# The small products of a mixer: from fifteen steps to five ordered groups per unit

## The chip, the core and the metric

The kernel runs on one core of a Trainium2 chip. A core has a matrix engine (TensorE, PE in the profile, with its weight loads as PEld), a vector engine (VectorE, DVE), a scalar engine (ScalarE, ACT), GpSimd (POOL) and SyncE (SP), which issues most DMAs. The engines run side by side and wait for one another through semaphores; each takes its own instructions in the order in which they were queued. The metric is the time of one execution on the device in microseconds (us), given as the median of several runs.

## What is computed

One step of a one-layer encoder on 1024 frames of a new stream (the prompt) and 32 frames of a running one (the sample). After a norm and an input projection, a mixer with three kinds of heads follows, then an output projection and a convolutional feed-forward part. The change lies in the mixer. Cut to what matters (L is 64 frames, 32 for the sample):

```python
# six heads of kind GLA (dk 32) and five of kind HGRN2 (dk 64), dv 64: per chunk of L frames
b = cumsum(log_a)
scores[i, j] = sum_d q[i, d] * k[j, d] * exp(b[i, d] - b[j, d])     # j <= i
o = scores @ v + (q * exp(b)) @ S
S = exp(b_last) * S + (k * exp(b_last - b)).T @ v
...
# five heads of kind mLSTM (dk 64): per chunk
s = (q @ k.T) * w                                                  # w: stabilised decays
num, den = s @ v + w0 * (q @ C), sum(s) + w0 * (q @ n)
C, n = dc * C + (wk * k).T @ v, dc * n + sum(wk * k)
```

## The kernel before

The 1056 frames are cut into nine units: units 0 to 7 are 128 prompt frames each (two chunks of 64), unit 8 is the 32 sample frames. Three groups of units, (0, 1, 2), (3, 4, 5) and (8, 6, 7), go through `inproj` (L357) one after the other. Its large products are done in three passes with the operands split into a high and a low half (`mm3`, L100 to L103, so that these three lines stand for all large products). The mixer of a group's units (`mixer`, L722) is a generator; `merge` (L1654) takes steps of it between the steps of the next group's `inproj`, and those of the last group between the steps of `outproj` (L1027). So the small products of a mixer lie between large products of another part, and NMIX (L1667) tells `merge` how many steps of a mixer to count for each unit. The yields inside `mixer` are these steps.

The instructions are put in order at build time by a planner: for each engine it takes, among those that it holds to be ready, the one with the lowest place in the program. `tc.high_priority(offset=n)` sets an instruction's place n lower than where it was written; the helper `first` (L718) does this with AHEAD = 100 for nearly all small products, which therefore all carry the line L720 in the profile. `tc.issue_after(ins)` queues the instructions of its block behind `ins` on that engine; it sets an order and adds no wait. In the profile, then, a small product is known by its output tile and not by its line.

A unit goes through these steps. (1) The loads. (2) qz (the queries times exp(b)), dec and kh (keys of the state update), and four transposes of kh through the tile mi into kt2 (L794 to L800). (3) One step for each of six levels c = 32, 16, 8, 4, 2, 1 (L825; five levels for unit 8): the scores between the two halves of each block of 2c frames. A level takes a difference and two exponentials into x (L836 to L845, NX = 3 buffers), products into Ld and Qz (L841 to L853, two buffers each), 16 matmuls into the PSUM tile sc (L856 to L863, one buffer of two banks), and a masked copy into P (`put`, L810; an ACT copy for the first level). With the last level go the four products of the diagonal (sd, L873 to L876). (4) The state update: for each chunk eleven products into mi (`up`, L882 to L893). (5) The outputs: P times v and qz times S into og and oh (L896 to L907). (6) `finish` (L917): norm and gate. (7) The mLSTM scores (sm, L937 to L947). (8) Transposes of its keys (kp, L950 to L958, into kw2) and the update of C (um, L963 to L972). (9) Its outputs: oi and om (L976 to L981), then division, `finish` and the store.

In PSUM, mi is one bank in two halves that `small` (L243) hands out in turn; the tiles og, oh, sm, om and oi share two buffers (tag "o"); the large products share three banks (tag "big", pool psb).

A product of 64 rows and 64 columns takes a quarter of the 128x128 array; the profile writes this as `64*64`, rows by columns of the array. The small products have these shapes: sc `64*64` (the first level `64*32`), kh, sd and the first kp `128*128`, up `128*32` (GLA) and `128*64` (HGRN2), og and oh `64*64` with P and `128*64` with S, sm `128*64` and `64*64`, the last kp `64*128`, um and oi `128*64`, om `64*64`. Each product of a 32-bit tile, transposes apart, stands in the profile as two instructions.

Two more places are touched. `back` (L448) in `vg_across` turns blocks of the last group's projection with transposes, for one unit at a time. `rows` (L550) makes the row factors of the mLSTM and turns them into columns (L599 to L622), in pieces from the tile mi for the second and third group.

Of the kernel before, what the change touches and what calls it, by code (L numbers as in the profile page):

```python
# [91 lines left out]
def body(ctx: ExitStack, tc: tile.TileContext, a: dict):  # L92
# [264 lines left out]
    def inproj(g, xh, xl, normed, scaled=None):  # L357
# [88 lines left out]
        def vg_across(blks):  # L446

            def back(blk, fs, part):  # L448
                for (u, off, n) in units_of(g)[part]:
                    ps = psb.tile([128, 256], F32, tag="big", name=f"pb{u}_{blk}")  # L450
                    for e in range(2):
                        pe.transpose(ps[:n, 128 * e:128 * e + 128], fs[e][:, off:off + n], ident)
                    vg_store(blk, u, off, n, ps)

            before = None
            for blk in blks:
# [3 lines left out]
                for e in range(2):  # L460
                    ps = psb.tile([128, T], F32, tag="big", name=f"pv{g}_{blk}_{e}")
                    for k in range(8):
                        mm3(ps, [w[:, 128 * e:128 * e + 128] for w in ws[k]], (xh[:, k, :], xl[:, k, :]), k == 0, k == 7)
                    act.copy(fs[e], ps)
                    if before:
                        back(*before, slice(e, 1 + 2 * e))
                    yield
                before = (blk, fs)
                yield
            for e in range(2):  # L470
                back(*before, slice(e, 1 + 2 * e))
# [78 lines left out]
        def rows():  # L550
# [48 lines left out]
            own = psm.tile([128, 4, 128], F32, tag="o", name="rows0", bufs=2) if g == 0 else None  # L599
            dcp = small(3, 8) if g else own[:, 3, :24].rearrange("p (a b) -> p a b", b=8)  # L600
            for f in range(3):
                pe.matmul(dcp[:, f, :ci], self_[R, 128 * f:128 * f + 128], dc[R, :ci], start=True, stop=True)
            dcs = mx.tile([128, 3, 8], F32, tag="dcs", name=f"dcs{g}", bufs=2)
            cl = mx.tile([128, 3, 128], F32, tag="cols", name=f"cols{g}", bufs=2)
            if g:
                with tc.high_priority(offset=AHEAD):
                    act.copy(dcs[:, :, :ci], dcp[:, :, :ci])
            for i0, i1 in ((0, 3),) if g == 0 else ((0, 2), (2, 3)):
                if g:
                    yield  # L610
                pt = own[:, :3] if g == 0 else small(i1 - i0, 128)
                for i in range(i0, i1):
                    u, off, n = us[i]
                    pe.transpose(pt[:n, i - i0, :], st[:, off:off + n], ident)
                n = us[i0][2]
                with tc.high_priority(offset=AHEAD):
                    act.copy(cl[:n, i0:i1], pt[:n, :i1 - i0])
                for i in range(i0, i1):
                    cols_of[us[i][0]] = cl[:, i]
            if g == 0:  # L620
# [97 lines left out]
    def first(fn, *args, **kw):  # L718
        with tc.high_priority(offset=AHEAD):
            fn(*args, **kw)  # L720

    def mixer(u, g, ci0):  # L722
# [71 lines left out]
        for f0 in (0, 2):  # L794
            kps = small(2, 128)
            for f in (f0, f0 + 1):
                first(pe.transpose, kps[:n, f - f0, :], khf[:, f * n:f * n + n], ident)
            for ch, (o, m) in enumerate(chunks):
                with tc.high_priority(offset=AHEAD):
                    act.copy(kt2[o:o + m, ch, 128 * f0:128 * f0 + 256], kps[o:o + m].rearrange("p f n -> p (f n)"))  # L800
# [23 lines left out]
        li = 0  # L824
        for c in levels:  # L825
# [20 lines left out]
            li += 1  # L846
# [7 lines left out]
            sc = psm.tile([128, 1024], F32, tag="sc", name=f"sc{u}_{c}", bufs=1)  # L854
            sc = sc[:, :11 * SCW].rearrange("p (h s) -> p h s", s=SCW)
            for j in range(4):  # L856
                for (o, m) in chunks:
                    for hf in range(2):
# [3 lines left out]
                        first(pe.matmul, sc[o:o + mm, p0:p0 + q1 - q0, :m // 2], L[r, f, o:o + mm],  # L862
                              Q[r, q0:q1, o // 2:(o + m) // 2], start=True, stop=True)  # L863
            if c == levels[0]:
                for (o, m) in chunks:
                    act.copy(P[o:o + c, :, c:2 * c], sc[o:o + c, :, :c])
            else:
                put(c, sc[:n, :, :cl // 2])
            if c == 2:

                z = mx.tile([128, 512], F32, tag="x", name=f"x{u}_0", bufs=NX)
                dve.tensor_tensor(z[:, :4 * n], q4.rearrange("p f n -> p (f n)"), k4.rearrange("p f n -> p (f n)"), op=ALU.mult)
                sd = small(11)  # L873
                for f in range(4):
                    first(pe.matmul, sd[:n], z[:, f * n:f * n + n], of_head[:, f, :], start=f == 0, stop=f == 3)
# [3 lines left out]

        og = psm.tile([128, 6, 64], F32, tag="o", name=f"og{u}", bufs=2)  # L880
        oh = psm.tile([128, 5, 64], F32, tag="o", name=f"oh{u}", bufs=2)
        Ss = []  # L882
        for ch, (o, m) in enumerate(chunks):
            S = state["S", u == 8]
            Ss.append(S)
            up = small(4, 64)
            for (f, r0, dk, vc) in HEADS:
                first(pe.matmul, up[r0:r0 + dk, f, :], kt2[:n, ch, 128 * f + r0:128 * f + r0 + dk], v[:n, vc:vc + 64],
                          start=True, stop=True)
            Sn = mx.tile([128, 4, 64], F32, tag="S", name=f"S{u}_{ch}", bufs=3)  # L890
            dve.tensor_tensor(Sn, S, dec[:, :, ch:ch + 1].broadcast_to([128, 4, 64]), op=ALU.mult)
            si = dve.tensor_tensor(Sn, Sn, up, op=ALU.add)
            state["S", u == 8] = Sn  # L893
        yield

# [1022 lines left out]
```

## Time and profile before

| | |
|---|---|
| three runs | 1376.77, 1379.4 (median), 1380.69 us |
| the profiled execution | 1378.88 us |
| its span, first to last instruction | 1377.1 us |
| granted TensorE clock, mean | 0.989 |
| instructions of PE | 11472 matmuls |

The profile's page has, for each engine, the busy time and its share of the span; the span in 40 slices; the DMA queues; the chain of work that ended last; and the costliest groups of instructions. Views of the trace answer narrower questions: the instructions in order of time, the groups within a window, what an engine waited for, and the busy time by stage. The mixers' products lie between 153 and 650 us; what follows (the feed-forward part) isn't touched. A matmul's duration is its time from issue to the end of its results, and matmuls overlap: what one costs the engine is read from the starts of those that follow it.

### The profile page before, as it was taken

The page shows a single profiled execution, that of the slowest core. Times are in us where ns is not written, and L with a number is a line of the kernel's source. Part 1 is how long each engine was busy: PE and PEld are TensorE (multiplying, and loading weights), DVE is VectorE, ACT ScalarE, POOL GpSimd, SP SyncE. Part 2 cuts the span into 40 slices and gives each one's busy share as a digit, 9 for nine tenths or more (in the row PEclk, how much of TensorE's full clock was granted, in tenths as well). Part 3 has the DMA queues.
Part 4 walks back from the last instruction along what each step waited for, and adds up shares of the span by engine and source line. Part 5 has one row for each costly group of instructions (what it writes and reads, how often), then busy time and mean ns, then how long its engine had stood idle before and what let it go on. Part 6 is the DMA issues. An engine that isn't in the chain of part 4 may idle for free.

```text
span 1377.1 us, 29219 instructions
## 1 busy us (share of the span) xinstructions
PE 1326.5 (96%) x11472; PEld 1198.8 (87%) x11472; DVE 1029.4 (75%) x1916; ACT 705.0 (51%) x1369; POOL 313.1 (23%) x529
## 2 busy tenths in 40 slices
PE   6999999999999898999989999999999999999997
PEld 5999889898889786867879999999999997678885
DVE  4786458768587669685989888888888876399566
ACT  4555447445475547342665555555455545454552
POOL 5532411226012154222211112111121110010005
PEclk9999999999999999999999999999999999999998
DMA  9699778876789936543423565655374239744435
GB/s 342 203 318 363 262 243 284 260 262 207 262 261 316 336 96 198 176 130 88 168 66 116 163 177 136 150 141 156 107 184 129 87 113 394 274 152 133 147 110 123
DMA packets 125825, 269.72 MB, mean 196 GB/s; under 512 B 24007, under 2 KB 59367, under 8 KB 125607
## 3 DMA queue, kind: packets, MB, share of 16 engines
q1 hardware_dynamic: 111959, 245.43, 52.9%
q0 software_dynamic: 8928, 18.09, 7.1%
q10 hardware_dynamic: 4800, 4.33, 0.9%
q8 instruction: 90, 1.47, 0.4%
q14 instruction: 48, 0.39, 0.1%
HBM read 206.72 MB, written 86.18 MB: 213 GB/s over the span
## 4 chain that ended last, share of the span: by engine, by line
PE 75%; DVE 10%; DMA 6%; ACT 5%; issue 2%; POOL 1%; SPq 1%; DVEq 0%; ACTq 0%; POOLq 0%
PE pux L101 4%; PE pux L102 4%; PE pux L103 4%; PE pv L101 4%; PE pv L103 4%; PE pv L102 4%; PE puw L102 3%; PE puw L103 3%; PE puw L101 3%; PE q L101 3%; PE q L102 3%; PE q L103 3%; PE x L101 2%; PE x L102 2%; PE x L103 2%; PE zp L101 2%
## 5 line engine op out<-in xcount | busy, mean ns | idle before, releaser
L1341 DVE SCALAR_TENSOR_TENSOR y<-uu,fconv_sb,y 128x1060 f32<-128x1060 f32 x88 | 116.2, 1321 | 36.7 <-ACT y L1339 35.8
L1277 ACT COPY c<-pux 128x272 f32<-128x272 f32 (+1 forms) x132 | 49.3, 376 | 50.1 <-PE pux L103 46.5
L101 PE MATMUL pv<-wt_0h,xh 128*128 128x256 f32 (+2 forms) x195 | 57.7, 296 | 5.4 <-ACT xh L321 4.8
L1339 ACT ACTIVATE y<-uu,fconv_sb 128x1060 f32<-128x1060 f32 x44 | 56.1, 1274 | 12.1 <-POOL uu L1335 10.8
L101 PE MATMUL zp<-woh,ch 128*128 128x512 f32 (+1 forms) x144 | 59.4, 414 | 2.4 <-DVE z L1156 1.2
L1338 POOL COPY fhalo<-uu 128x2 f32<-128x2 f32 x44 | 17.1, 388 | 184.2 <-DVE uu L1282 184.2
L102 PE MATMUL zp<-wol,ch 128*128 128x512 f32 (+1 forms) x144 | 57.9, 402 | 0.0
L103 PE MATMUL zp<-woh,cl 128*128 128x512 f32 (+1 forms) x144 | 57.8, 402 | 0.0
L103 PE MATMUL pv<-wt_1h,xl 128*128 128x256 f32 (+2 forms) x195 | 57.1, 293 | 0.0
L103 PE MATMUL pv<-wt_0h,xl 128*128 128x256 f32 (+2 forms) x195 | 56.7, 291 | 0.4 <-DVE xl L322 0.4
L101 PE MATMUL pv<-wt_1h,xh 128*128 128x256 f32 (+2 forms) x195 | 56.9, 292 | 0.0
L102 PE MATMUL pv<-wt_1l,xh 128*128 128x256 f32 (+2 forms) x195 | 56.8, 291 | 0.0
L102 PE MATMUL pv<-wt_0l,xh 128*128 128x256 f32 (+2 forms) x195 | 56.2, 288 | 0.1
L1517 POOL TENSOR_TENSOR gss<-gss 128x1 f32<-128x1 f32 (+1 forms) x9 | 8.1, 899 | 186.8 <-ACT gjk L1510 186.8
L220 POOL TENSOR_SCALAR hrs<-hss 128x5 f32<-128x5 f32 (+3 forms) x27 | 9.6, 356 | 161.2 <-DVE hss L922 159.8
L101 PEld LDWEIGHTS pv<-wt_0h,xh 128*128 128x128 f32 (+1 forms) x195 | 36.8, 189 | 7.4 <-ACT xh L321 5.7
L431 POOL TENSOR_TENSOR vg<-vth,gh 128x256 f32<-128x256 f32 (+1 forms) x36 | 29.2, 812 | 61.6 <-DMA vm<-v_d 22.0
L815 DVE COPY_PREDICATED P<-masks_sb,sc 128x352 f32<-128x352 int32 (+1 forms) x44 | 29.8, 677 | 11.8 <-PE sc L720 11.5
L851 DVE TENSOR_TENSOR Qz<-x,qe 128x128 f32<-128x128 f32 (+1 forms) x106 | 29.8, 298 | 11.7 <-PE sc L720 11.0
L103 PEld LDWEIGHTS pv<-wt_0h,xl 128*128 128x128 f32 (+1 forms) x195 | 37.1, 190 | 1.2 <-DVE xl L322 0.9
L101 PEld LDWEIGHTS pv<-wt_1h,xh 128*128 128x128 f32 (+1 forms) x195 | 37.6, 193 | 0.4 <-issue 0.2
L103 PEld LDWEIGHTS pv<-wt_1h,xl 128*128 128x128 f32 (+1 forms) x195 | 37.4, 192 | 0.6 <-issue 0.2
(1718 smaller groups left out, 5384.3 us busy)
## 6 DMA issues: line engine op xcount, KB each, us to landing
wrP<-in_w_dn SPq DMA_DIRECT2D x27, 512.0 KB, 3.4
h_d<-y SPq DMA_DIRECT2D x22, 530.0 KB, 2.8
ht<-h_d SPq DMA_DIRECT2D x22, 530.0 KB, 8.8
wt_0r<-in_w_tok SPq DMA_DIRECT2D x21, 512.0 KB, 5.2
wt_1r<-in_w_tok SPq DMA_DIRECT2D x21, 512.0 KB, 6.8
ws_d<-in_w_dn POOLq DMA_DIRECT2D x20, 512.0 KB, 8.7
wrP<-ws_d SPq DMA_DIRECT2D x20, 512.0 KB, 4.2
wt_0l<-lt_d SPq DMA_DIRECT2D x14, 512.0 KB, 4.1
```

What stands on the lines that cost most here:

```text
L101: pe.matmul(ps, lh[0], rh[0], start=first, stop=False, **kw)
L102: pe.matmul(ps, lh[0], rh[1], start=False, stop=False, **kw)
L103: return pe.matmul(ps, lh[1], rh[0], start=False, stop=last, **kw)
L220: pool.tensor_scalar(out, ss, 1.0 / width, eps, op0=ALU.mult, op1=ALU.add)
L431: pool.tensor_tensor(o[:n], th[:n], gh[:n, c0:c0 + 256], op=ALU.mult)
L815: dve.copy_predicated(dst, mk.broadcast_to([n, 11, *mk.shape[2:]]), src)
L851: dve.tensor_tensor(Qp[:, 2 * i, :, :n // 2].rearrange("p e (m c) -> p e m c", c=c), second(x4[:, f:f + 1], c).broadcast_to([128, 2, n // ...
L1277: kept[name] = act.copy(t, ps)
L1338: behind["POOL"] = pool.tensor_copy(fhalo[:, j, :], u[:, NCOL - 2:NCOL])
L1339: act.activation(y, u, AF.Identity, scale=fconv[:, j, 2:3], bias=fconv[:, j, 3:4])
L1341: dve.scalar_tensor_tensor(y, uu[i][:, s:s + NCOL], fconv[:, j, s:s + 1], y, op0=ALU.mult, op1=ALU.add)
L1517: pool.tensor_tensor(ss[:n, 0:1], ss[:n, 2:3], ss[:n, 3:4], op=ALU.add)
```

## The change

Each unit's small products are queued in five groups, each a chain in a fixed order. `soon` replaces `first`: its offset is 400, and each product is queued behind the product before it. Two levels share one tile sc, and the level that is made last comes first; its results are stored side by side (`at`). With the first pair of levels go the transposes of kh, with the second the mLSTM's scores and key transposes, with the third the diagonal and the state update of both chunks; then og and oh with the update of C; then oi and om. The yields of a unit fall from fifteen to nine, and NMIX from 17 to 11. `back` turns all three units of a block at once, in two PSUM tiles; `rows` does its products in one piece in a tile of its own in all groups.

```diff
-            def back(blk, fs, part):
-                for (u, off, n) in units_of(g)[part]:
-                    ps = psb.tile([128, 256], F32, tag="big", name=f"pb{u}_{blk}")
+            def back(blk, fs):
+                us = units_of(g)
+                whole = psb.tile([128, 2, 256], F32, tag="big", name=f"pb{us[0][0]}_{blk}")
+                rest = psb.tile([128, 256], F32, tag="big", name=f"pb8_{blk}")
...
+            own = (psb if g else psm).tile([128, 4, 128], F32, tag="big" if g else "o", name=f"rows{g}", bufs=3 if g else 2)
...
-    def first(fn, *args, **kw):
-        with tc.high_priority(offset=AHEAD):
-            fn(*args, **kw)
+    SOON = 400
+    line = [None]
+    def soon(fn, *args, **kw):
+        with tc.high_priority(offset=SOON), tc.issue_after(line[0].ins) if line[0] else ExitStack():
+            line[0] = fn(*args, **kw)
...
+        def scores(sc, c, L, Q, at):
+            for j in (3, 0, 1, 2):
...
+                        soon(pe.matmul, sc[o:o + mm, p0:p0 + q1 - q0, at:at + m // 2], L[r, f, o:o + mm],
+                             Q[r, q0:q1, o // 2:(o + m) // 2], start=True, stop=True)
...
+        for l0 in range(0, len(levels), 2):
+            pair = [operands(c, i) for i, c in enumerate(levels[l0:l0 + 2])]
+            last_pair = pair[-1][0] == levels[-1]
+            if last_pair:
                 z = mx.tile([128, 512], F32, tag="x", name=f"x{u}_0", bufs=NX)
...
+            if l0 == 2:
+                act.copy(mqz[0:64, 0:5:2, :n], mq[0:64, :, :])
...
+            sct = psm.tile([128, 1024], F32, tag="sc", name=f"sc{u}_{l0}", bufs=1)
...
+            line[0] = None
+            for i in reversed(range(len(pair))):
+                scores(sc, *pair[i], i * (cl // 2))
+            sd = sct[:, 11 * SCW:11 * SCW + 11]
+            if l0 == 0:
+                keys()
+            elif l0 == 2:
+                memory_scores()
+            if last_pair:
                 for f in range(4):
-                    first(pe.matmul, sd[:n], z[:, f * n:f * n + n], of_head[:, f, :], start=f == 0, stop=f == 3)
+                    soon(pe.matmul, sd[:n], z[:, f * n:f * n + n], of_head[:, f, :], start=f == 0, stop=f == 3)
+                si = states()
+            for i, (c, L, Q) in enumerate(pair):
...
+                    put(c, sc[:n, :, at:at + cl // 2])
...
         og = psm.tile([128, 6, 64], F32, tag="o", name=f"og{u}", bufs=2)
         oh = psm.tile([128, 5, 64], F32, tag="o", name=f"oh{u}", bufs=2)
...
+        line[0] = None
...
+        memories()
...
+        line[0] = None
+        for h in range(5):
+            for ch, (o, m) in reversed(list(enumerate(chunks))):
+                soon(pe.matmul, oi[o:o + m, h, :], mqz[:, h, o:o + m], Cs[ch][:, h // 2, :], start=True, stop=True)
...
-    NMIX, NIN = 17, 12 + 2 + 24
+    NMIX, NIN = 11, 12 + 2 + 24
```

The functions `keys`, `memory_scores`, `states` and `memories` hold the lines of before for kt2, for sm with w and kp, for `up` with S, and for um with C; the products of both chunks come first in the last two, and the sums on VectorE behind them.

207 lines of the change are left out of this document (98 added, 109 removed).

## The prediction, made before the changed kernel ran

> **What bounds the kernel now.** I read the page first, for the engine that is full and for the chain that ended last:
>
> ```profile
> span 1377.1 us, 29219 instructions
> PE 1326.5 (96%) x11472; PEld 1198.8 (87%) x11472; DVE 1029.4 (75%) x1916; ACT 705.0 (51%) x1369; POOL 313.1 (23%) x529
> ...
> PE 75%; DVE 10%; DMA 6%; ACT 5%; issue 2%; POOL 1%; SPq 1%; DVEq 0%; ACTq 0%; POOLq 0%
> ```
>
> PE is busy for 96% of the span, and three quarters of the chain are its own work. [...] So the second view is the stages in which mixers run, and in them the small products alone:
>
> ```profile
> core 0: us, PE busy (x) PEld busy (x) DVE busy (x) ACT busy (x) POOL busy (x), PEclk, DMA share, GB/s
> 150.00:350.00 200.00, 195.86 (x2307) 179.31 (x2305) 142.20 (x330) 107.95 (x221) 52.02 (x76) 0.98 0.76 250
> 350.00:500.00 150.00, 144.46 (x1892) 129.71 (x1890) 106.65 (x284) 82.53 (x193) 32.01 (x52) 0.99 0.83 274
> 500.00:660.00 160.00, 152.77 (x1551) 118.77 (x1550) 120.37 (x258) 69.66 (x157) 51.70 (x80) 0.98 0.47 145
> ...
> 150.00:660.00 510.00, 141.14 (x3485) 112.42 (x3485) 0.98 0.69 224
> ```
>
> The last row is L720 alone: 3485 small products fill 141 of 510 us. In all three stages PE is idle for 2 to 5% of the time, VectorE for 25 to 29%. A microsecond of PE taken out of these 510 should therefore mostly come off the end, as long as the others can follow.
>
> What a small product costs isn't its duration, since many lie beside one another; it is read from the starts in the list of instructions in time. Here is one level of scores between large products (columns: start and duration in us, engine, line, operation, output from inputs, rows by columns of the array, size of the output, count):
>
> ```profile
> 305.60 0.28 PE L101 MATMUL pv<-wt_0h,xh 128*128 128x256 f32 x1
> 305.81 0.69 PE L720 MATMUL sc<-Qz,Ld 64*64 64x64 f32 x32
> 306.43 0.39 PE L102 MATMUL pv<-wt_0l,xh 128*128 128x256 f32 x1
> 306.66 0.28 PE L103 MATMUL pv<-wt_0h,xl 128*128 128x256 f32 x1
> 306.78 0.28 PE L101 MATMUL pv<-wt_0h,xh 128*128 128x256 f32 x1
> ```
>
> Large products follow each other by 0.12 us (306.66 to 306.78). From 305.60 to 306.66 pass 1.06 us; less two large steps of 0.12, the 32 products of the level cost 0.82 us. The first of them comes 0.21 us after the large one before it, and the second large one 0.23 us after the first: both edges are slow. A place where two shapes alternate gives the price of an edge:
>
> ```profile
> 598.55 0.56 PE L720 MATMUL om<-vm,w 64*64 64x65 f32 x10
> 599.04 0.56 PE L720 MATMUL mi<-vm,kw 128*64 128x65 f32 x10
> 599.53 0.33 PE L720 MATMUL om<-vm,w 64*64 64x65 f32 x2
> 599.79 0.33 PE L720 MATMUL oi<-C,mqz 128*64 128x65 f32 x2
> 600.05 0.33 PE L720 MATMUL om<-vm,w 64*64 64x65 f32 x2
> ```
>
> Ten products of one shape take 0.49 us, two take 0.26 us, each with one change of shape. Eight products more cost 0.23 us, 29 ns each, so the change alone costs 0.26 - 0.06 = 0.20 us. The level of scores gives a little less: four `64*64` products lie side by side where `128*64` has two, so 32 cost 32 x 14.5 ns = 0.46 us, and 0.82 - 0.46 leaves 0.18 us for each of its two changes. I take **0.18 us for a change of shape**, and keep 0.20 as the upper end.
>
> [...]
>
> **The change, part by part.** *Changes of shape.* Before, I counted them in the list in time. The second unit's mixer runs between these rows:
>
> ```profile
> 232.93 0.55 PE L720 MATMUL sc<-Qz,Ld 64*32 64x64 f32 x32
> 233.41 0.44 PE L101 MATMUL pf<-xh,wf_11h 128*128 128x384 f32 x1
> ...
> 284.67 0.64 PE L720 MATMUL oi<-C,mqz 128*64 128x65 f32 x16
> 285.24 0.39 PE L102 MATMUL pv<-wt_1l,xh 128*128 128x256 f32 x1
> ```
>
> with 37 changes, the third's from 289 to 343 us with 40, and between 150 and 660 us there are 353 with a mixer's product on at least one side: 39 a unit over nine units. After, from the code: the first group is `64*64`, `64*32`, `128*128` (three changes, since transposes have the shape of the large products). The second is `64*64` for both levels, `128*64` and `64*64` (sm), `128*128` and `64*128` (kp): six. The third is `64*64`, `128*128` (sd), and `128*32`, `128*64` twice (up): seven. The fourth is `64*64`, then `128*64` for S and um together: three. The fifth is `128*64`, `64*64`: three. That is 22 a unit, 198 in all, and 155 fewer: 155 x 0.18 = **27.9 us**.
>
> *Broken groups.* The planner puts a large product in between wherever an item of the chain isn't ready. sm needs two ACT copies, up needs kt2, qz times S needs the state after the first chunk. That the level made last comes first means that both are ready when the chain begins, and oi begins with the chunk whose C is late. No row shows how often groups break. It lies between no extra change and all 17 saved in a unit; I take three a unit, nearest to the clean count: 27 x 0.18 = **4.9 us** given back.
>
> *Waits of PE.* The places where PE, at a small product, waits for an engine:
>
> ```profile
> its engine sat idle before it (us, times) until:
>   issue: 14.9, 70
>   DVE Qz L851: 4.8, 7
>   DVE kh L793: 3.2, 2
>   DVE P L815: 2.8, 7
>   DVE kw L957: 2.7, 6
> ```
>
> The four rows with a name sum to 13.5 us in 22 waits. I leave them as they are (0), with half gained (7 us) and the slow rival below as the two ends.
>
> *Order on the other engines.* Nothing is added to VectorE or ScalarE; the work on w, kw2 and C moves ahead of the last levels and of `finish`. On VectorE that is (behind the bar: busy us in all, mean ns of one, then its idle time)
>
> ```profile
> L957 DVE TENSOR_TENSOR kw<-mi,cols 64x256 f32<-64x256 f32 (+1 forms) x8 | 2.6, 319 | 4.9 <-PE mi L720 4.9
> ...
> L947 DVE TENSOR_TENSOR w<-w,sm 128x320 f32<-128x320 f32 x2 | 1.0, 480 | 0.0
> ```
>
> four of kw and one of w, 4 x 0.32 + 0.48, with two more operations of w of the same size: 2.7 us a unit ahead of the last pair's copies into P. I cost them at nothing: large products cover them while any are left, and VectorE has 40 of 160 us free in the fullest stage. Without that cover they are 2.7 x 9 = 24 us. Loads gain a little: mqk and ab are free sooner, so SP can load the next unit's earlier; 0, since no wait for them stands above.
>
> *PSUM.* `back` holds two of the three large banks at once, seven times, and `rows` one, twice. PE waited 0.3 us at L101 for such a store (ACT vg L419), once:
>
> ```profile
> PE pv L101 <- ACT vg L419: 0.3, 1, 0.3
> ```
>
> Nine times 0.3 is 2.7 us, nine times nothing is the other end; I take **2.0 us** lost. Two levels in one sc tile cost nothing more than one level did: both have one buffer.
>
> The sum: 27.9 - 4.9 - 2.0 = **21.0 us** less, so the profiled execution of 1378.88 us (its span of 1377.1 and 1.8 around it) becomes 1357.9. The median stands 0.5 us above it: **1358 us**.
>
> **The rivals.** *Slower: the fixed order holds PE up.* A pair's scores begin only when both levels' operands are done, where before the first level's scores lay beside the making of the second's. A level's operands on VectorE are
>
> ```profile
> L847 DVE TENSOR_TENSOR Qz<-x,qkb x9: 272/277/1098, 551.3 to 616.0; 128x128 f32<-128x128 f32 x9
> L841 DVE TENSOR_TENSOR Ld<-x,qkb x7: 399/409/422, 552.0 to 611.9; 128x256 f32<-128x256 f32 x7
> ...
> L836 DVE TENSOR_TENSOR x<-qkb x5: 674/686/691, 583.9 to 602.4; 128x512 f32<-128x512 f32 x5
> ```
>
> (medians in the middle), with three of Qz's size: 0.69 + 0.41 + 3 x 0.28 = 1.94 us. There are 26 pairs (unit 8 has a last level alone): 50 us if PE stands still for all of it. Past 21 / 50 = 42% of that the change loses; at 70% it gives 1358 + 35 = 1393 us. For it: the planner places a product by times of its own, and offset 400 puts a whole group ahead of all large products. Against it: large products are there to be put first, and the 53 levels of now have only 7 waits for Qz, 4.8 us.
>
> *Part of it is taken by others.* Data moves at 93% of the queues' time in one stage:
>
> ```profile
> 402.00:448.00 46.00, 44.15 (x577) 40.60 (x576) 37.59 (x97) 26.53 (x63) 9.51 (x20) 0.96 0.93 305
> ```
>
> and VectorE is at 75% in the last. If the three units of the second group gain nothing (7 us) and those of the last half (3.5 us), it is 1368 us. Against it: the PE waits quoted are for engines, none for a transfer.
>
> *More than that.* At 0.20 us a change, no broken groups and half the waits gone, 155 x 0.20 + 7 = 38 us: 1341 us.
>
> *No gain.* Either the change doesn't do what it says, because the planner breaks the chains as often as before, or a change of shape costs nothing in itself and the slow edges belong to each entry of a small product between large ones: 1379 us. [...] The alternating rows, 0.26 us a pair with no large product near, speak against the second, the offset of 400 against the first.
>
> **How the numbers follow.** Forecast (1350 to 1366): 0.52. More: 0.12. Part: 0.13. No gain: 0.08 (0.06 for broken groups, 0.02 for a change of shape that is free). Slower: 0.15. A measurement of this kernel can tell about 0.3%, 4 us, from no change. Faster by over 0.3% is forecast, more and part: 0.77; within: 0.08; slower: 0.15. The range leaves out the slow rival and the far ends of more and of no gain: 1341 to 1378 us; the high end is the bound with every broken group, the low end the one at 0.20 a change.
>
> **What would show it.** Right: some 200 changes of shape between 150 and 660 us; 64 score products in one row; om and oi no longer alternating; the mixers' end near 630 us instead of 650; the feed-forward part as long as before. The price is wrong if the changes fall and the mixers' stage doesn't. The prediction is wrong if PE's idle time before small products rises by 20 us (for Qz or P: the slow rival), if waits for transfers appear on ScalarE where weights are split (part), or if large products stand inside the groups (no gain).

## The result, and the profile after

The changed kernel takes 1396.45 us (median of 6 runs, 1394.8 to 1400.45), the kernel before 1378.61 us beside it (6 runs, 1376.77 to 1382.14): **slower by 1.3%**, ratio 1.0132 with a 95% interval of 1.0111 to 1.0153. The forecast was 1358 us. The profiled execution of the changed kernel took 1395.19 us. Its page, in the lines that answer to those of before (span; busy time, share and instructions of each engine; the chain of work that ended last):

```profile
span 1393.4 us, 29184 instructions
...
PE 1316.8 (95%) x11472; PEld 1197.7 (86%) x11472; DVE 1022.0 (73%) x1916; ACT 704.4 (51%) x1368; POOL 329.2 (24%) x529
...
PE 72%; DVE 12%; DMA 6%; ACT 5%; issue 2%; POOL 2%; SPq 0%; DVEq 0%; ACTq 0%; POOLq 0%
```

PE is busy for 9.7 us less than before (1326.5) and the span is 16.3 us longer: PE works less and stands still more. The three stages with mixers, in the view of busy time by stage:

```profile
150.00:350.00 200.00, 189.32 (x2333) 177.16 (x2332) 141.13 (x330) 101.86 (x207) 54.08 (x75) 0.97 0.75 248
350.00:500.00 150.00, 135.06 (x1723) 123.19 (x1722) 100.59 (x280) 81.74 (x193) 34.59 (x49) 0.94 0.78 264
500.00:660.00 160.00, 143.32 (x1502) 114.61 (x1501) 111.43 (x243) 69.91 (x156) 61.17 (x79) 0.95 0.47 151
```

PE's busy times sum to 467.7 of 510 us where they were 493.1, and the granted clock (the column behind POOL) has fallen from 0.98 or 0.99 to 0.94 to 0.97. The groups themselves are as the code has them. The fourth group of a unit, in the list of instructions in time:

```profile
161.74 0.91 PE L719 MATMUL og<-v,P 64*64 64x64 f32 x24
162.49 0.75 PE L719 MATMUL oh<-v,P 64*64 64x64 f32 x20
163.17 0.92 PE L719 MATMUL og<-S,qz 128*64 128x64 f32 x24
163.92 0.75 PE L719 MATMUL oh<-S,qz 128*64 128x64 f32 x20
164.50 0.86 PE L719 MATMUL mi<-vm,kw 128*64 128x65 f32 x20
```

108 matmuls pass with one change of shape among them. Counted in that list from 120 to 700 us, changes with a mixer's product on at least one side fall from 353 to 239. What the new order cost stands in the view of the mixers' line, where PE sat idle ahead of a small product (its matmuls alone, without the weight loads):

```profile
its engine sat idle before it (us, times) until:
  DVE cat L992: 16.5, 9
  DVE P L807: 2.7, 3
  ACT kt L868: 2.2, 2
```

The largest rows of the same view of the kernel before:

```profile
  DVE Qz L851: 1.9, 2
  DVE kh L793: 1.5, 1
  DVE P L815: 1.0, 3
```

From 60 us to the feed-forward part these waits sum to 7.0 us before and 22.5 after. (The rows of 13.5 us in the prediction come from the same view with weight loads in it, where one wait can stand twice.) Others wait too; the view of PE's waits (total, times, longest):

```profile
PE pv L101 <- ACT xh L321: 6.2, 5, 3.0
PE ctp L1076 <- DVE vth L429: 3.8, 1, 3.8
PE zp L101 <- DVE z L1185: 2.9, 2, 2.6
```

These are large products and transposes. pv waits for an input (xh) from ScalarE; ctp and zp wait for PSUM banks that VectorE has yet to empty (vth belongs to the store of `back`). PE's waits ahead of products other than the mixers' sum to 13.2 us before and 24.3 after, over the same stretch.

To put sizes on this I split the time from 60 us to the first product of the feed-forward part (665.8 us before, 683.3 after; what follows takes 711.3 and 710.1 us; of the 17.5 us, 13.6 stand already where the last pv begins, at 522.7 against 509.1 us) by the starts in PE's list. Between two large products, more than 0.15 us beyond their usual step is standstill; beside a small product, more than 0.4 us is. The rest is work. The trace also lists when the clock was granted at half (0.50): 17 us of this time before, 44 after; half of it, less the standstill in it, is an estimate of what it lost, and work less this loss is work at the full clock.

| kernel | changes of shape | standstill | work | lost to half clock | work at full clock |
|---|---|---|---|---|---|
| before | 353 | 22.1 | 583.6 | 8.3 | 575.3 |
| after | 239 | 50.2 | 573.0 | 20.9 | 552.1 |
| difference | -114 | +28.1 | -10.6 | +12.6 | -23.2 |

So the saving came: 23.2 us of PE's work for 114 changes. It was paid back twice, by 28 us of standstill and by 13 us of half clock. The split is an estimate, from one execution of each kernel. With other cut-offs, and with all idle time inside the half-clock stretches taken off, the same lists give 20 to 22 us of work, 27 to 29 of standstill and 10 of half clock; their sum, 17.5 us, stays. The mean granted clock of the kernel before lies between 0.981 and 0.989 over the 47 executions beside the experiments, so one execution can lose some 5 us more or less to half clock than the middle of this range, by an estimate from it (0.004 of 1377 us).

**One wait, followed back.** PE, VectorE (DVE), ScalarE (ACT) and GpSimd (POOL) around the longest one, from the list in time (the bracket is the idle time before, and what ended it):

```profile
470.32 0.82 PE L455 MATMUL pb<-ident,vf 128*128 128x128 f32 x6
...
472.44 0.96 ACT L814 ACTIVATE qe<-qkb,cf_sb 128x32 f32<-128x32 f32 x4 [8.47 <-DMA qkb<-qkbs_d]
...
473.30 0.47 ACT L989 ACTIVATE sq<-og 128x384 f32<-128x384 f32 x1
...
473.80 0.55 DVE L990 TENSOR_REDUCE hss<-sq 128x6 f32<-128x384 f32 x1 [9.88 <-ACT sq L989]
...
474.44 0.20 POOL L220 TENSOR_SCALAR hrs<-hss 128x6 f32<-128x6 f32 x1 [19.86 <-DVE hss L990]
...
476.71 0.55 DVE L992 TENSOR_TENSOR cat<-og,hrs 128x384 f32<-128x384 f32 x1
...
477.35 0.39 ACT L468 COPY vf<-pv 128x288 f32<-128x288 f32 x1
477.40 0.89 PE L719 MATMUL oi<-C,mqz 128*64 128x65 f32 x11 [6.26 <-DVE cat L992]
```

Read it from below. oi stands at the head of PE's queue and needs the bank that og leaves when cat is made. cat waits for the norm (hrs), that for the sums (hss), those for the squares (sq), and sq stands in ScalarE's queue behind qe of the next unit, which waited 8.47 us for its load. What ended the wait at its far end is that load; four engines' queues pass it on, and PE stands for 6.3 us with large products queued behind oi. Those couldn't have filled the time: of the three large banks, pv's is emptied by vf at 477.35 us and the two of `back` (pb) after that, both on ScalarE, behind the same qe.

### The profile page after: what moved, and what is told of

The parts are those of the page before. It is cut to its first block, busy times and chain, and to the rows that moved or that the text cites. A ratio compares the mean times of both kernels' runs of the same rounds, so it can differ in the third digit from the quotient of the medians.

```text
span 1393.4 us, 29184 instructions
## 1 busy us (share of the span) xinstructions
PE 1316.8 (95%) x11472; PEld 1197.7 (86%) x11472; DVE 1022.0 (73%) x1916; ACT 704.4 (51%) x1368; POOL 329.2 (24%) x529
## 4 chain that ended last, share of the span: by engine, by line
PE 72%; DVE 12%; DMA 6%; ACT 5%; issue 2%; POOL 2%; SPq 0%; DVEq 0%; ACTq 0%; POOLq 0%
PE pux L103 4%; PE pux L102 4%; PE pux L101 4%; PE pv L101 3%; PE puw L102 3%; PE puw L101 3%; PE puw L103 3%; PE pv L103 3%; PE pv L102 3%; PE q L101 3%; PE q L102 3%; PE q L103 3%; PE x L101 2%; DMA qkb<-qkb_d 2%; PE x L102 2%
## 5 line engine op out<-in xcount | busy, mean ns | idle before, releaser
L1367 POOL COPY fhalo<-uu 128x2 f32<-128x2 f32 x44 | 16.5, 376 | 178.6 <-DVE uu L1311 178.5
L220 POOL TENSOR_SCALAR hrs<-hss 128x5 f32<-128x5 f32 (+3 forms) x27 | 13.0, 483 | 179.4 <-DVE hss L990 178.5
L807 DVE COPY_PREDICATED P<-masks_sb,sc 128x352 f32<-128x352 int32 (+3 forms) x53 | 38.0, 716 | 17.7 <-PE sc L719 16.5
L102 PEld LDWEIGHTS pv<-wt_0l,xh 128*128 128x128 f32 (+1 forms) x195 | 37.6, 193 | 0.8 <-POOL wt_0l L110 0.5
L221 POOL TENSOR_TENSOR hrs<-hrs,mhalf 128x5 f32<-128x5 f32 (+3 forms) x27 | 37.7, 1395 | 2.3
```

The source lines that it names most:

```text
L102: pe.matmul(ps, lh[0], rh[1], start=False, stop=False, **kw)
L220: pool.tensor_scalar(out, ss, 1.0 / width, eps, op0=ALU.mult, op1=ALU.add)
L221: pool.tensor_tensor(out, out, mhalf[:n, :cols], op=ALU.pow)
L807: dve.copy_predicated(dst, mk.broadcast_to([n, 11, *mk.shape[2:]]), src)
L1367: behind["POOL"] = pool.tensor_copy(fhalo[:, j, :], u[:, NCOL - 2:NCOL])
```

## The experiments

All times are medians beside the kernel before on the same chip (its medians are 1378.6 to 1380.5 us), ratios are to it.

**Is it the order of the products?** First the chains alone are taken away (the products keep offset 400):

```diff
-        with tc.high_priority(offset=SOON), tc.issue_after(line[0].ins) if line[0] else ExitStack():
+        with tc.high_priority(offset=SOON):
```

> The changed kernel without the chains: offset 400, the planner free to put the products of a group in any order. If the chains make PE wait: fewer waits, more changes of shape, 1375 to 1388 us. If the offset does: the waits stay and changes of shape are added, 1396 to 1405 us.

1442.18 us, ratio 1.0460 (1.0433 to 1.0487), far above both expectations. The shapes mix, as the list in time shows:

```profile
263.46 0.33 PE L719 MATMUL mi<-vm,kw 128*64 128x65 f32 x2
263.72 0.33 PE L719 MATMUL og<-v,P 64*64 64x64 f32 x2
263.97 0.33 PE L719 MATMUL mi<-vm,kw 128*64 128x65 f32 x2
```

Two matmuls take 0.26 and 0.25 us (263.46 to 263.72 to 263.97), as where shapes alternated before the change. There are 467 changes of shape, 228 more than with chains, and 594.1 us of work at the full clock, 42 more: 0.18 us each. The fixed order is worth 46 us at this offset. It isn't free: by the view of waits PE stands still for 30 us without the chains and for 47 with them. But without them there are also 85 us of half clock, where the changed kernel has 44. Then the shapes alone are made worse, P and S alternating by head in the fourth group:

```diff
         for (h0, h1, ot) in ((0, 6, og), (6, 11, oh)):
             for h in range(h0, h1):
...
-        for (h0, h1, ot) in ((0, 6, og), (6, 11, oh)):
-            for h in range(h0, h1):
-                f, r0, dk, vc = HEADS[h]
                 for ch, (o, m) in enumerate(chunks):
                     soon(pe.matmul, ot[o:o + m, OUT[h], :], qz[:, h, o:o + m], Ss[ch][:, f, :],
```

> The changed kernel, but in the fourth group the products with P (64*64) and with S (128*64) alternate head by head: the same products, 20 more changes of shape in each of nine units, 180 in all. If a change of shape costs 0.18 us wherever it stands: 32 us more, about 1428 us. If only the edges to large products cost: 1396 us as before.

1403.29 us, ratio 1.0173 (1.0148 to 1.0198). 186 more changes (425) give 25 us more work at the full clock (577.4), 0.14 us each. That lies between the two expectations. The kernel is only 7 us slower than the changed one, since the standstill falls from 50 to 38 us. PE has time to spare in the changed kernel: work added to it lies partly in its waits, and so does work saved.

**Is it the shared banks?** oi and om get the two banks of sc, so that they wait for no norm:

```diff
-        om = psm.tile([128, 5, 65], F32, tag="o", name=f"om{u}", bufs=2)
-        oi = psm.tile([128, 5, 65], F32, tag="o", name=f"oi{u}", bufs=2)
+        both = psm.tile([128, 1024], F32, tag="sc", name=f"oo{u}", bufs=1)
+        oi = both[:, :325].rearrange("p (h d) -> p h d", d=65)
+        om = both[:, 512:837].rearrange("p (h d) -> p h d", d=65)
```

> The changed kernel, but oi and om get the two banks of the sc tile instead of the two banks that og and oh leave. Theory (PE stands still at oi and om because these banks come free only after the norm of og and oh; 17.7 us of waits, and the half clock that follows them): the waits on the cat operation vanish, about 18 to 25 us less than the changed kernel, so 1371 to 1379 us. Rival (the level pairs make PE wait, or the planner's order as such): no change from 1396 us, or slower because the next unit's scores now wait for oi and om to be read.

1395.92 us, ratio 1.0122 (1.0098 to 1.0146): nothing gained, and the theory that these banks are the loss falls. PE's waits between 60 and 700 us:

```profile
PE pv L103 <- DVE xl L322: 7.7, 3, 4.7
...
PE sc L719 <- DVE Qz L841: 3.7, 2, 3.2
```

The waits for cat are gone and others of the same sum have come (46.3 us in all by the view of waits, 46.8 in the changed kernel), most of them of large products. Two more parts were put back one at a time. `back` as in the kernel before (one unit at a time, one bank):

```diff
-            def back(blk, fs):
+            def back(blk, fs, part):
...
-                    if before and e:
-                        back(*before)
+                    if before:
+                        back(*before, slice(e, 1 + 2 * e))
```

> The changed kernel, but the transposes of the last group's projection are done for one unit at a time as in the kernel before. If holding two of the three large banks at once makes PE wait (in the changed kernel it waits 6 us at pb and ctp for the stores): 4 to 8 us less, 1388 to 1392 us. If not: 1396 us.

1394.0 us, ratio 1.0110 (1.0090 to 1.0131), which isn't told apart from the changed kernel. And the mLSTM's scores, keys and state behind `finish`, as one more group:

```diff
-            elif l0 == 2:
-                memory_scores()
...
+        line[0] = None
+        memory_scores()
+        memories()
```

> The changed kernel with the mLSTM's scores, key transposes and update of C back behind the norm of og and oh, as one group of their own (24 changes of shape a unit instead of 22, about 3 us). If moving this work ahead of the last levels and of the norm makes the others late: 1380 to 1390 us. If not: 1396 to 1400 us.

1402.5 us, ratio 1.0172 (1.0145 to 1.0200): worse by some 6 us, for which 30 more changes of shape (269) are enough at 0.18 us each. Their early place isn't the harm.

**Is it the offset?** The kernel before with one number changed, and no group formed:

```diff
     def first(fn, *args, **kw):
-        with tc.high_priority(offset=AHEAD):
+        with tc.high_priority(offset=400):
```

> The kernel before with an offset of 400 in place of 100 for its small products, nothing else. If the offset makes PE wait: 10 to 25 us more than the kernel before, 1389 to 1404 us. If not: within 4 us of the kernel before, or a few us less because its products split less.

1399.17 us, ratio 1.0164 (1.0131 to 1.0197). Changes of shape (351) and work at the full clock (573.6 us) are as before; the standstill rises from 22 to 38 us and the loss to half clock from 8 to some 14 to 17. The largest rows of PE's waits:

```profile
PE sc L720 <- ACT P L866: 7.2, 1, 7.2
PE pv L101 <- ACT xh L321: 5.8, 2, 3.8
PE sc L720 <- DVE P L815: 2.9, 2, 1.7
```

A level's scores now stand at the head of PE's queue and wait for sc to be emptied into P (10.1 us in three waits), and large products wait more, too (21.2 us in all against 13.2). So the offset alone does as much harm to the kernel before as the whole change. The other way round, the changed kernel with offset 100:

```diff
-    SOON = 400
+    SOON = 100
```

> The changed kernel with an offset of 100 in place of 400 for all its groups; order and chains stay. Theory (the offset pulls whole groups, and with them the mixer's work on VectorE and ScalarE, ahead of what the large products wait for): waits and half clock fall most of the way back to those of the kernel before while the changes of shape stay low, so 1362 to 1378 us. Rival (the fixed chains are what makes PE wait, wherever the groups stand): 1390 to 1397 us.

1390.04 us, ratio 1.0086 (1.0053 to 1.0119), the rival's figure. With offset 100 for the fifth group alone:

```diff
-                soon(pe.matmul, oi[o:o + m, h, :], ..., start=True, stop=True)
+                soon(pe.matmul, oi[o:o + m, h, :], ..., start=True, stop=True, by=AHEAD)
...
```

> The changed kernel, but the products of the fifth group (oi, om) are set only 100 places forward, not 400. If PE stands still there because the offset puts the group ahead of large products that could run, the waits shrink by more than half: 1380 to 1388 us. If the planner believes the banks to be free earlier than they are, whatever the offset, the waits stay: 1393 to 1398 us.

1389.36 us, ratio 1.0075 (1.0046 to 1.0104). Both give back 6 to 7 us, over a third of the loss; the second lies between its two expectations. Offset 100 and banks of their own together, by the two diffs above:

> The changed kernel with offset 100 and with oi and om in the two banks of the tile sc, so that they wait for no output of the norms. Theory that two kinds of wait stand side by side (groups set too early, and the shared output banks): each alone gave 0 to 6 us, both together give more than the sum, 1375 to 1382 us. Rival, that the order of the work on VectorE and ScalarE is late in itself, whatever the banks: 1388 to 1391 us, as with offset 100 alone, and the waits turn up at other products.

1392.24 us, ratio 1.0084 (1.0061 to 1.0107): the two don't add up; the standstill is 46 us with either bank.

**Are the groups' own operands late?** In the next two the scores read the loaded keys and qz in place of Ld and Qz, and P times v reads qz in place of P (the operands are still made); first on the changed kernel with oi and om in sc's banks, then on the kernel before:

```diff
-... L[r, f, o:o + mm], Q[r, q0:q1, o // 2:(o + m) // 2], ...
+... k4[r, f, o:o + mm], qz[r, q0:q1, o // 2:(o + m) // 2], ...
...
-... P[o:o + m, PLANE[h], :m], v[o:o + m, vc:vc + 64], ...
+... qz[o:o + m, h, :m], v[o:o + m, vc:vc + 64], ...
```

> As the changed kernel with oi and om in the tile sc's banks, but the scores read the loaded keys and qz in place of Ld and Qz, and P times v reads qz in place of P, so that these products have inputs made long before; the operands are still made, on the same engines, and PE does the same number of products of the same shapes. What is left out: the outputs are not the reference's. Theory, that the waits for operands took the gain: stalls fall by 20 us or more, 1360 to 1370 us, and it stands some 15 to 20 us below the same edit of the kernel before. Rival, that the fewer changes of shape are worth nothing in time, or that other work got longer: within 5 us of that edit, or above it.

> The kernel before with the same edit (scores from the loaded keys and qz, P times v from qz; outputs not the reference's). It had few waits for these operands, so both theories expect 1370 to 1378 us; it is the mark for the run above.

1410.86 us, ratio 1.0227 (1.0209 to 1.0245), and 1399.72 us, ratio 1.0144 (1.0125 to 1.0162). Both missed: the edit made both kernels slower, for a cause that I can't name, and the groups stay behind by 11 us although they do some 30 to 36 us less work at the full clock (by the split above 546.7 against 583.1, with 245 changes of shape against 387; by the other cut-offs 30 us). Their standstill is 62 us against 29, and it stands elsewhere:

```profile
PE pv L101 <- ACT vf L468: 7.6, 4, 5.7
PE zp L101 <- DVE cl L1082: 6.4, 1, 6.4
PE pv L101 <- DVE xl L322: 5.3, 1, 5.3
```

The theory that the waits are for the groups' operands finds no support, though a kernel that the edit slows by other ways is no clean test of it. Here the large products wait for what ScalarE and VectorE make for them (cl, xl) or have to take out of their banks (vf).

**Is it the steps?** A mixer of before has fifteen steps a unit and one of after nine, each with the operands of two levels, so VectorE's work is written in larger lumps between the pieces of the large part. An extra step between a pair's operands and its scores, with offset 100:

```diff
+            yield
             sct = psm.tile([128, 1024], F32, tag="sc", name=f"sc{u}_{l0}", bufs=1)
...
-    NMIX, NIN = 11, 12 + 2 + 24
+    NMIX, NIN = 14, 12 + 2 + 24
```

> The changed kernel with offset 100 and one more step between the making of a pair's operands and its products (a yield ahead of each pair's scores, NMIX 14): each group is written about a third of a large block later than its operands. Theory that PE stands still because a group is placed when the planner believes its inputs to be ready and the chip has them later: stalls of PE fall from 47 to 30 us or less, 1370 to 1380 us. Rival, that the inputs are late because VectorE and ScalarE are: the extra step only moves the wait, 1388 to 1395 us.

1393.49 us, ratio 1.0086 (1.0059 to 1.0113): no gain over offset 100 alone, but the loss has one place. Its input projection ends at 508 us (509 in the kernel before), and its output projection's stage then takes 173 us against 157. There PE waits like this (the row of ScalarE makes ch, the input of cl):

```profile
538.38 2.43 DVE L783 TENSOR_TENSOR qz<-qkb,eb 32x256 f32<-32x256 f32 x6
538.63 0.56 ACT L1081 CAST ch<-ctp 128x512 fp32r<-128x512 f32 x1
540.84 1.29 DVE L1157 SCALAR_TENSOR_TENSOR z<-z,oss,gm 128x1024 f32<-128x1024 f32 x1
542.04 0.42 DVE L904 TENSOR_TENSOR S<-S,dec 128x256 f32<-128x256 f32 x1
542.38 0.69 DVE L792 TENSOR_TENSOR kh<-kh,qkb 128x512 f32<-128x512 f32 x1
542.98 0.47 DVE L1015 TENSOR_TENSOR hn<-hn,om 32x325 f32<-32x325 f32 x1
543.38 0.47 DVE L936 TENSOR_TENSOR w<-ab,cols 128x320 f32<-128x320 f32 x1
543.78 0.67 DVE L1082 TENSOR_TENSOR cl<-ctp,ch 128x512 fp32r<-128x512 f32 x1
...
544.51 0.80 PE L103 MATMUL zp<-woh,cl 128*128 128x512 f32 x1 [4.53 <-DVE cl L1082]
```

VectorE works without a break for over 5 us. cl, which the large product needs, stands last, behind qz, S, kh, hn and w of the mixers and one product of the projection (z). Its input ch is there at 539.19 us, so it isn't late for its input: for 4.6 us it stands behind other work. The projection's own copies and sums were then given offset 400 on ScalarE and VectorE:

```diff
-            with tc.high_priority(offset=AHEAD):
+            with tc.high_priority(offset=400):
                 ins = (act.copy(ch[:, :, :n], ps[:, :, :n]),
...
+            with tc.high_priority(offset=400):
                 act.activation(z[:n, cs[hf]], ps[:n], AF.Square, accum_out=ss[:n, hf:hf + 1])
...
```

> The run with offset 100 and a step between operands and scores, with one edit: the output projection's own work between products (ch and cl, the copies of zp into z, the two sums into z and x) has offset 400 on ScalarE and VectorE, so that it stands ahead of the mixers' work there. Theory that PE waits for these because they stand behind the mixers' work: the stage falls from 173 to some 160 us, 1378 to 1384 us, and the waits for cl and z go. Rival, that they are late because their own inputs are: 1390 to 1396 us.

1397.41 us, ratio 1.0131 (1.0097 to 1.0164), above both expectations. It doesn't put the theory to the test: cl stands behind the same operations as before (at 544.12 us), so the offset didn't move it. That fits a planner that takes the lowest place only among what it holds to be ready. The steps by themselves, in the kernel before (no yield after the first level of a pair, after the state update, after sm and after um; NMIX 11):

```diff
-            yield
+            if li % 2 == 0 or c == levels[-1]:
+                yield
...
-    NMIX, NIN = 17, 12 + 2 + 24
+    NMIX, NIN = 11, 12 + 2 + 24
```

> The kernel before with nine steps a unit (no yield after the first level of a pair, after the state update, after sm and after um; NMIX 11), its products in the order and with the offset of before. Theory of lumps: 1385 to 1393 us, with waits of PE for the large products' inputs, though no group was formed. Rival, that the groups and not the steps make the loss: 1377 to 1382 us.

1388.58 us, ratio 1.0068 (1.0047 to 1.0088): the figure that the theory of lumps gave, but not its mechanism. By the view of waits PE stands still for 21.8 us (20.2 in the kernel before), 12.1 of them at large products (13.2), so the waits that the theory expected aren't there. What grew in the profile is half clock, from 17 to 34 us, and that varies from one execution to another: over this kernel's four executions the mean granted clock lies between 0.982 and 0.985, within the range of the kernel before. Why the steps cost time here stays open. And the changed kernel with offset 100 and fifteen steps (the yield ahead of the scores, and one between the two levels of a pair; NMIX 17):

```diff
-            pair = [operands(c, i) for i, c in enumerate(levels[l0:l0 + 2])]
+            pair = []
+            for i, c in enumerate(levels[l0:l0 + 2]):
+                if i:
+                    yield
+                pair.append(operands(c, i))
```

> The changed kernel with offset 100 and fifteen steps a unit as in the kernel before (a yield between the two levels of a pair and one ahead of each pair's scores, NMIX 17): the groups of products stay, but VectorE's work for two levels is no longer written in one lump. Theory of lumps, that the large products' own inputs wait on VectorE and ScalarE behind two levels at a time: the output projection's stage falls from 173 to 160 us or less, 1366 to 1380 us. Rival, that the lump isn't the cause but the order or the late groups: 1385 to 1395 us.

1387.06 us, ratio 1.0052 (1.0033 to 1.0072): the output projection's stage falls to 157.2 us (161.4 with offset 100 and nine steps), as expected of it, but the whole stays above the 1380 us that this theory gave at most and lies where the rival had it. Offset 100 with the extra step beside the input projection, and offset 400 (100 for the fifth group) without it beside the output projection:

```diff
-        with tc.high_priority(offset=SOON), ...
+        with tc.high_priority(offset=by if GROUP[0] == 2 else AHEAD), ...
...
+            if g < 2:
+                yield
             sct = psm.tile([128, 1024], F32, tag="sc", name=f"sc{u}_{l0}", bufs=1)
```

> The changed kernel with offset 100 and a step between operands and scores for the units that run beside the input projection, and offset 400 (100 for the last group of a unit) without that step for the three that run beside the output projection. From the stage times of two runs (up to 508 us in the one, 152 us for the output projection's stage in the other) the theory that the two stages want different places gives 1370 to 1378 us; the rival, that a stage only looked short because work had been done ahead of it, 1385 to 1393 us.

1383.4 us, ratio 1.0038 (1.0022 to 1.0054). It is the best of the versions with groups and no gain: 5 us above the most that the stage times had promised, just below the rival's range.

**What is left?** With fifteen steps and offset 100, PE's waits between 60 and 700 us begin with

```profile
PE oi L719 <- DVE cat L997: 6.3, 3, 4.0
PE om L719 <- DVE cat L997: 3.8, 3, 1.9
```

so oi and om were given sc's banks here too (the diff of the first such run):

> The changed kernel with offset 100, fifteen steps a unit, and oi and om in the two banks of sc, which takes away the 10 us in which PE waits for cat. Theory that the waits at the shared banks are what is left: 1374 to 1380 us. Rival, that the waits move on to the next product, since VectorE is late in any case: 1384 to 1390 us.

1386.12 us, ratio 1.0045 (1.0026 to 1.0065), the rival's figure, and the waits are others again:

```profile
PE oo L719 <- DVE C L923: 5.7, 2, 3.5
PE sc L719 <- DVE Qz L841: 3.9, 2, 3.8
```

With `back` as before on top of it (its diff is above, too):

> The same, and `back` turns one unit at a time in a bank of its own, as in the kernel before. Theory that holding two of the three large banks holds up the large products in the last part of the third group: 2 to 5 us below the run above. Rival, that it does nothing there, as with offset 400: within 2 us of it.

1393.4 us, ratio 1.0103 (1.0081 to 1.0126): worse by 7 us, against both expectations, where the same edit did nothing at offset 400. I have no cause for it: its profiled execution, 1388.57 us, is the fastest of its six, and shows 8 us more standstill, spread over many waits.

## Why the prediction was wrong

**What held.** *Changes of shape* and *Broken groups* together forecast 225 changes and 23.0 us; there are 239, and 23.2 us of work at the full clock went (20 to 22 by the other cut-offs). The price of 0.18 us was right beyond these two kernels: over eleven of them (before, after and nine experiments, 239 to 467 changes), a straight line through work at full clock against changes of shape has a slope of 0.184 us, with single kernels up to 8 us off it. The 14.5 ns for a score product held as well: 64 in one row, from 155.26 to 156.32 us in the changed kernel, take 1.06 us, which less one change is 13.8 ns each; other `64*64` products took longer (24 of og with P in 0.75 us, 31 ns each). The feed-forward part is as long as before, and the mixers' last product starts at 641 us where it was near 648 (630 was forecast for the mixers' end). For *PSUM* I put 2.0 us: in the changed kernel PE waits 5.9 us for the store of `back` (ctp 3.8, pb 2.1), but with `back` as before (e4) the time can't be told from that of the changed kernel.

**What failed** are two steps that I put at nothing. *Waits of PE*: "I leave them as they are (0)". The standstill rose by 28 us, over half of it at small products (7.0 to 22.5 us) and the rest at large ones. The 13.5 us that I started from counted weight loads as well; matmuls alone waited 7.0 us, so half of them gained would have been 3.5 us and not 7. Another 10 to 13 us went to half clock, for which the sum has no term at all. *Order on the other engines*: "I cost them at nothing: large products cover them". The large products covered nothing where they waited for the same queues: their inputs (cl, xl, xh) are made, and their banks emptied (vf, z), by VectorE and ScalarE, as the mixers' operands are, and PE's waits ahead of products other than the mixers' rose from 13.2 to 24.3 us. I looked at VectorE's average, 40 of 160 us free, and not at what stands ahead of a given operation; in the example above, from the run with offset 100 and one more step, it was 4.6 us of other work, most of it the mixers', ahead of 0.7 us that PE waited for.

**The slower rival** had the sign and nearly the size (1393 us), but not the place. It had PE stand for Qz and P until a pair's operands are done. Those waits are few in the changed kernel (P 2.7 us, Qz none; cat has 16.5), and with inputs that are ready (f3) the standstill didn't fall. Its sign was 20 us more idle time before small products, for Qz or P; there were 15.5, most of it for cat. That it came near the time is in part luck. What I held against the rival, that large products are there to be put first, is where I was wrong: at 471 us all three large banks were waiting for ScalarE, too.

**The loss by parts**, in one order of adding them: groups (with the new `back` and `rows`), offset 100 and fifteen steps, 1.0052; nine steps, 1.0086; offset 400, 1.0132. That is about 7, 5 and 6 us. The intervals of neighbours overlap, so the shares aren't settled by this row alone; in the kernel before nine steps cost 0.68% and offset 400 1.64%, both clear of nothing. The parts don't add: the offset is worth 20 us without groups and 6 with them.

**What stays open** is why the groups, at the offset and with the steps of before, still cost more waits than they save work: in the profiled execution of g1 (1381.6 us, the fastest of its eight), by the split above 18.7 us less work at the full clock, 14.5 us more standstill, 8.5 us more lost to half clock, 4.3 us in all. Each wait at the shared banks that was taken away came back at other products (e1, f1, i1). That fits a kernel that is bound by the round trip between PE, ScalarE and VectorE in fixed queues, and not by PE's work, but no run here shows such a bound by itself.

## What to carry to other kernels

Here an engine that was 96% busy was the bound only as long as its inputs came in time: with 9.7 us less of busy time on PE the span grew by 16.3 us. Before taking work off such an engine, ask of the next product in its queue, large or small, who makes its input and what stands ahead of that. When one edit bundles a new order, an offset and a coarser stepping, price each by itself in the old kernel: here the order's saving came out within some 3 us of the forecast, and the offset alone, one number in the old kernel, lost as much as the whole change. A wait that is taken away is a gain only if the time falls; three times here it came back at another product.

## What the runs showed of the hardware

In the changed kernel half clock mostly stood beside a standstill: seven of its eight stretches between 60 us and the feed-forward part begin in a wait of PE of 1.5 us or more, or at most 2.1 us behind it; the eighth, at 553.1 us, begins 2.4 us behind one of 0.90 us. At 252 us PE waited 2.55 us for cat:

```profile
251.22 0.80 PE L719 MATMUL oi<-C,mqz 128*64 128x65 f32 x20
254.57 0.80 PE L719 MATMUL om<-vm,w 64*64 64x65 f32 x20 [2.55 <-DVE cat L992]
```

and the busy time of each engine in the stretches around it (the 0.50 is the granted clock):

```profile
252.00:256.00 4.00, 1.45 (x25) 1.39 (x25) 4.00 (x9) 0.92 (x3) 2.10 (x3) 1.00 0.11 42
256.30:259.50 3.20, 3.20 (x11) 3.20 (x11) 3.20 (x11) 3.10 (x6) 0.54 (x1) 0.50 0.71 195
259.70:263.00 3.30, 3.30 (x21) 3.30 (x20) 3.30 (x8) 2.32 (x5) 0.71 (x2) 1.00 0.73 214
```

VectorE is busy for 4.00 of 4.00 us, with the next unit's operands among it, while PE waits for its cat. Then PE, full again, runs 3.4 us at half clock (11 matmuls in 3.2 us, then 21 in 3.3). Between 60 us and the feed-forward part the kernel before has five such stretches, all of 3.4 us, and the changed one eight, five of them of 6.8 us.

Length alone didn't decide. In the same trace an idle time of PE of the same 2.55 us, ahead of 595.41 us, has no half clock behind it, and one of 1.53 us, ahead of 612.47 us, has 6.8 us. Half clock also came without any standstill. In the run without chains shapes had alternated for 5 us when it set in at 162.5 us (the columns as above):

```profile
159.10:162.50 3.40, 3.40 (x29) 2.52 (x28) 0.00 (x0) 0.00 (x0) 0.00 (x0) 0.99 0.53 188
162.50:176.10 13.60, 13.60 (x89) 11.25 (x88) 4.13 (x6) 2.03 (x6) 0.00 (x0) 0.50 0.28 89
```

PE is busy for 3.40 of 3.40 us, and yet 13.6 us at half clock follow. So the 0.18 us, which are counted at the full clock, may not be all that such a row of changes cost, and the half clock of the changed kernel need not all come from its standstills. No run here separates the two.
